# A hybrid decoder layer: ranking the mixer's hops and the evictions, and moving four ties and loads

## The chip, the cores and the metric

The kernel is one program on one core of a Trainium2 chip. Time is the device time of one execution in microseconds, the median of repeated runs. The core has five engines with queues of their own: TensorE (PE, matmuls into PSUM; its weight loads are shown as PEld), VectorE (DVE), ScalarE (ACT), GpSimd (POOL) and SyncE (SP), which here issues nearly every DMA. Instructions of one engine run in the order in which they stand in its queue. Semaphores order the engines among each other.

## What is computed

One decoder layer on 2048 tokens of width 1024, in float32:

```python
mod = jax.nn.silu(c) @ w_ada + b_ada
shift1, scale1, gate1, shift2, scale2, gate2 = jnp.split(mod, 6, axis=-1)
h = modulate(rmsnorm(x, norm1_w), shift1, scale1)
q, k, v, z, xbc, dt = split(h @ w_in)
attn = sliding_window_attention(rope(q), rope(k), v, sinks)      # 8 heads, window 128
xbc = silu(causal_depthwise_conv(xbc, conv_w, conv_b))           # 4 taps
y = ssd_chunked_scan(xs, softplus(dt + dt_bias), A, B, C, d_skip) # 16 chunks of 128, a state carried
y = grouped_rmsnorm(y * silu(z)) * ssm_norm_w
x = x + gate1 * (concat(attn, y) @ w_out)
h = modulate(rmsnorm(x, norm2_w), shift2, scale2)
x = x + gate2 * ((silu(h @ w_gate) * (h @ w_up)) @ w_down)
return rmsnorm(x, final_norm_w)
```

## The kernel before

**Numbers.** Each float32 factor of a projection is split into a high half, rounded to fp32r (ACT, a copy), and a low half (DVE, the difference). A product is then three matmuls, hi x hi, hi x lo and lo x hi (`mm3`, L281 to L284). Weights are loaded to `raw`, split into `w` (six buffers), and for later blocks the split form is kept in DRAM.

**Blocks and projections.** The tokens are worked in four blocks of 512, b = 0 to 3. For each block the stage before the feed-forward part runs, one after another on PE: `queries`, `keys_values`, `convolved` (8 columns of 128 channels) and `gated`. Each computes into a PSUM bank `d` (four of them, from `dense()`), and evicts: `query` and `key_value` apply the rotary angles (`rope`, DVE and POOL) and store to DRAM; `gate` applies silu and stores; `convolved` evicts a column by a copy of the bank with its three halo columns (L510), two scaled copies on ACT (L513, L514), two multiply-adds on DVE (L515, which reads the bank, and L516) and a sum on POOL (L517). The tail of a column, `end` (L491 to L494: a Tanh, a multiply-add and the store of the column), is traced half a column later.

**The mixer beside them.** `attentions(b)` and `ssds(b)` are generators. One step of them, between two yields, is a hop: a few small matmuls or transposes on PE in banks am, at, sm and st, and the vector work that answers them. `tick` (L1473) advances such a side generator by a given ratio between the steps of the main one. Their results go to DRAM (`spill`). In `attentions` a hop is, in turn: transposes of k and q (L611, L616), scores and their maxima (L651, L660), the softmax (L669 to L679), its transposes (L685, L687) and the product with v (L694, L696). In `ssds` it is: transposes of x (L752), the product of B and C (L759), decays (L723 to L728), the state's output (L785), the new state (L794), the output (L806 to L809), a root mean square whose inverse square root takes some fifteen tiny instructions on DVE and POOL (L815, `rsqrt` at L246), and, hops later, the scaling on ACT (L734), the transposes (L739) and the store (L742, L743). They load q, k, v, z and x of the next 128 tokens on SP one tile ahead (L599, L600, L702, L703).

**Other work in the same queues.** `norm1` of the next block loads x twice (L363, and L345 in `load_x`), squares it on ACT (L364), and makes the operands `hl` (L337, L339, L340). `ada_later` computes the rest of `mod` by reductions on DVE (L204). `mixed(b)` loads the mixer's result from `spill` (L831) and splits it into halves (L837 on ACT, L839 on DVE). `out_proj(b)` multiplies it by w_out, adds x (L858), stores (`mid`, L859) and sums squares. It loads x of column c + 1 in the middle of column c.

**The feed-forward part.** Gate and up projection are done by a Strassen-like scheme: `quads(s)` for token blocks 2s and 2s + 1, 22 quads of seven products each (L1034 to L1036), with operands made by `operands_first`, `operands_between`, `sums_ahead`, `operands_kept` and `operands_last`. The down projection follows the same scheme (`steps_of`, L1166; its token operands `a` at L1147 and L1148, its weights at L1161 and L1162). During the first quads the hops of blocks 2 and 3 run as sides; then `first_output` and `second_output` project blocks 2 and 3, and `first_operands` and `last_operands` run as sides too.

**Order.** A scheduler at build time goes through the traced instructions with a model of the machine. On each engine it takes, of those that are ready in the model, the one of the lowest rank. The rank is the place in the trace. On PE the order is the traced one from the opening through the last projection of block 3; from the first quad on PE is ranked as well. Inside `tc.manual_schedule` other engines named there keep the traced order too. `tc.issue_after(i)` ties what is traced in it behind instruction i in the queue of i's engine, without a wait for its end; `behind(engine)` (L189) ties to the last instruction traced on that engine. In the kernel before, `mixed` ties both halves of its split in this way.

Of the kernel before, what the change touches and what calls it, by code (L numbers as in the profile page):

```python
# [18 lines left out]
P = 128  # L19
# [12 lines left out]
RAW, SPLIT = 5, 6  # L32
TMP, M1, M2, M4 = 8, 3, 8, 4
MIX, MIX2, MIX1, RATIO_UP = 0.78, 1.1, 1.25, 0.75
HALF = 32
ROPE_THETA = 10000.0
TWO_PI_1 = 6.25
# [7 lines left out]
def hymba_layer(ctx, tc, xT, xtok, pos, wada, wadk, vecs, rows, wq, wkv, wz, wx, wo, wgu, wd, outT):  # L45
# [139 lines left out]
        nc.vector.scalar_tensor_tensor(scl1[:, d:d + 2], mod[:, 8 + d:10 + d], 1.0, n1w[:, d:d + 2], ALU.add, ALU.mult)  # L185

    held_back = set()

    def behind(engine):  # L189
        traced = nc.cur_bb.bb.instructions  # L190
# [236 lines left out]
    def two_parts(b, h, name, src, done):  # L427

        store, banks = b == (0 if name == "z" else 1), [None, None]
        for kh in range(2):  # L430
            for part in range(2):
                if kh == 0:
                    banks[part] = [dense(), dense()]
                outs = [banks[part][t // 2][:, t % 2 * 256:t % 2 * 256 + 256] for t in range(NT)]
                for kp in (2 * kh, 2 * kh + 1):
                    whi, wlo = weight(src[part][kp], 512, (f"{name}{part}", kp), store)
                    for e in range(2):
                        k, cs = 2 * kp + e, slice(e * 256, (e + 1) * 256)
                        for t, out in enumerate(outs):
                            ts = slice(t * P, (t + 1) * P)  # L440
                            mm3(out, h[k][0][:, ts], h[k][1][:, ts], whi[:, cs], wlo[:, cs],
                                k == 0 and t % 2 == 0, k == KT - 1 and t % 2 == 1)
                    if kp % 2 == 0:
                        yield
                if kh:
                    for t, out in enumerate(outs):
                        done(part, t, out)
                yield

    def first_columns(h):  # L450
# [29 lines left out]
    def keys_values(b, h, halves=(0, 1), bank_of=lambda i: dense()):  # L480
        if b and 0 in halves:
            dt_of[b] = small([P, NT, 8], "dt", 3)
        for half in halves:
            for t, ps in (yield from tokens(b, h, "kv", wkv, 264, (2 * half, 2 * half + 1), bank_of)):
                key_value(b, t, ps)
            yield

    def convolved(b, h):
        ending = []

        def end(c, cv, th, o):  # L491
            nc.scalar.activation(th, cv, AF.Tanh)
            nc.vector.scalar_tensor_tensor(o, th, 1.0, cv, ALU.add, ALU.mult)
            nc.sync.dma_start(xs_d[b][c], o)  # L494

        for c in range(8):
            ps = dense()
            for half in range(2):
                if half:
                    if ending:  # L500
                        end(*ending.pop())
                    yield
                whi, wlo = weight(wx[c, half], T, ("x", c, half), b == 1)
                for i in range(4):
                    k = 4 * half + i
                    ws = slice(i * P, (i + 1) * P)
                    mm3(ps, whi[:, ws], wlo[:, ws], h[k][0], h[k][1], k == 0, k == KT - 1)
            cin = small([P, T + 3], "cin", 2, pool=ip)
            nc.gpsimd.tensor_copy(cin[:, 0:3], halo[:, c, :])
            nc.scalar.copy(cin[:, 3:T + 3], ps)  # L510
            nc.gpsimd.tensor_copy(halo[:, c, :], cin[:, T:T + 3])
            cv, th, o = big("s", 3, pool=fw), big("s", 3, pool=fw), big("sx", 2, pool=ip)
            nc.scalar.activation(cv, cin[:, 0:T], AF.Identity, scale=conv_w[:, c, 0:1], bias=conv_b[:, c:c + 1])  # L513
            nc.scalar.activation(th, cin[:, 1:1 + T], AF.Copy, scale=conv_w[:, c, 1:2])  # L514
            nc.vector.scalar_tensor_tensor(cv, ps, conv_w[:, c, 3:4], cv, ALU.mult, ALU.add)  # L515
            nc.vector.scalar_tensor_tensor(th, cin[:, 2:2 + T], conv_w[:, c, 2:3], th, ALU.mult, ALU.add)  # L516
            nc.gpsimd.tensor_tensor(cv, cv, th, ALU.add)  # L517
            ending.append((c, cv, th, o))
            if c == 7:
                end(*ending.pop())  # L520
            yield
# [305 lines left out]
    def mixed(b, mix, cs, into):  # L827
# [5 lines left out]

        def split():
            for n, (hi, lo) in enumerate(got):
                with behind(mybir.EngineType.Activation):
                    nc.scalar.activation(hi, lo.bitcast(F32), AF.Copy)  # L837
                with behind(mybir.EngineType.DVE):
                    nc.vector.tensor_tensor(lo, lo.bitcast(F32), hi.bitcast(F32), ALU.subtract)  # L839
                mix.append((hi, lo))  # L840
                if n % 2:
                    yield
        return split()

    def out_proj(b, y_of, mix, bank_of, acc, norm=None, each=lambda c: None):
        nxt = load_x(b, 0)
        for c in range(KT):
            ps, x = bank_of(c), nxt
            for half in range(2):
                if half:  # L850
                    nxt = load_x(b, c + 1) if c < KT - 1 else None
                    yield
                whi, wlo = weight(wo[c, half], T, ("o", c, half), b == 0, b > 1)
                for i in range(4):
# [618 lines left out]
    def tick(ratio):  # L1473
# [7 lines left out]
        due[0] += ratio  # L1481
        while due[0] >= 1.0:
            due[0] -= 1.0
            while sides and next(sides[0], sides) is sides:
                sides.pop(0)

    def beside(main, ratio):
        for i, _ in enumerate(main):
# [309 lines left out]
```

## Time and profile before

| what | us |
|---|---|
| median of three runs | 2225.2 (2223.36 to 2226.75) |
| the profiled execution | 2224.71 |
| its span, first to last instruction | 2223.0 |
| mean granted PE clock | 0.987 |
| POOL busy | 549.9 |
| opening, to the first projection on PE | about 36 |
| projections and mixer, blocks 0 to 3, up to the first quad | about 36 to 711 |
| first quads; the hops of blocks 2 and 3 beside them up to 1211 | about 711 to 1272 |
| output projections of blocks 2 and 3 | about 1218 to 1337 |
| first part of the down projection | about 1338 to 1434 |
| second quads | about 1435 to 1865 |
| the rest of the down projection and the final norm | about 1857 to 2223 |

A row of the stretches names an interval, its length, then busy time and number of instructions of each engine, then the granted clock of PE (1.00 is full), the DMA share and its rate. In a row of a timeline stand the start, the duration, the engine, the line, the operation, what it writes and reads, the shape, and in brackets how long the engine had been idle and what ended that. "SPq" is the issuing of DMAs in SP's queue. "w L882 <- PE d L1036: 226.7, 124, 4.8" would read: ACT waited for PE 226.7 us in total, 124 times, at most 4.8 us.

### The profile page before, as it was taken

The page shows a single profiled execution, that of the slowest core. Times are in us where ns is not written, and L with a number is a line of the kernel's source. Part 1 is how long each engine was busy: PE and PEld are TensorE (multiplying, and loading weights), DVE is VectorE, ACT ScalarE, POOL GpSimd, SP SyncE. Part 2 cuts the span into 40 slices and gives each one's busy share as a digit, 9 for nine tenths or more (in the row PEclk, how much of TensorE's full clock was granted, in tenths as well). Part 3 has the DMA queues.
Part 4 walks back from the last instruction along what each step waited for, and adds up shares of the span by engine and source line. Part 5 has one row for each costly group of instructions (what it writes and reads, how often), then busy time and mean ns, then how long its engine had stood idle before and what let it go on. Part 6 is the DMA issues. An engine that isn't in the chain of part 4 may idle for free.

```text
span 2223.0 us, 33256 instructions
## 1 busy us (share of the span) xinstructions
PE 2154.6 (97%) x10984; PEld 1775.6 (80%) x10984; DVE 1660.7 (75%) x3195; ACT 1017.4 (46%) x2135; POOL 549.9 (25%) x658
## 2 busy tenths in 40 slices
PE   8989999999899999999998999999999999999998
PEld 6879897778678677788887888788888888788887
DVE  6977856876568777688886878878878775786575
ACT  3664734743445555433343545533333333554451
POOL 0213443322102211144342221233232231110011
PEclk9989999999999999999999999999999999999999
DMA  7788988796899432333333587835555535778653
GB/s 271 248 306 279 353 263 282 255 320 198 305 339 357 150 106 86 104 119 105 125 122 119 199 296 252 279 125 166 189 162 187 168 118 202 257 261 271 180 170 102
DMA packets 287708, 466.76 MB, mean 210 GB/s; under 512 B 27440, under 2 KB 97072, under 8 KB 287536
## 3 DMA queue, kind: packets, MB, share of 16 engines
q1 hardware_dynamic: 286960, 464.13, 62.6%
q8 instruction: 86, 1.41, 0.3%
q14 instruction: 86, 0.70, 0.1%
q10 hardware_dynamic: 576, 0.52, 0.1%
HBM read 329.73 MB, written 134.81 MB: 209 GB/s over the span
## 4 chain that ended last, share of the span: by engine, by line
PE 88%; DVE 4%; DMA 4%; ACT 2%; issue 1%; POOL 0%; SPq 0%; DVEq 0%; ACTq 0%; POOLq 0%
PE d L1166 15%; PE d L1034 10%; PE d L1036 10%; PE d L1035 10%; PE d L282 7%; PE d L283 7%; PE d L284 7%; PE d L1307 1%; PE am L1036 1%; PE am L1034 1%; PE am L1035 1%; PE am L694 1%; PE sm L806 1%; DMA a<-act_t 1%; PE sm L1036 1%
## 5 line engine op out<-in xcount | busy, mean ns | idle before, releaser
L1166 PE MATMUL d<-a,w 128*128 128x512 f32 x1716 | 403.4, 396 | 3.8 <-DVE w L1162 2.0
L1166 PEld LDWEIGHTS d<-a,w 128*128 128x128 f32 x1716 | 321.7, 188 | 82.6 <-DVE w L1162 2.9
L1034 PE MATMUL d<-b,w 128*128 128x512 f32 x924 | 365.6, 400 | 4.4 <-ACT b L916 2.1
L1035 PE MATMUL d<-b,w 128*128 128x512 f32 x924 | 367.3, 397 | 0.3 <-DVE b L917 0.2
L1036 PE MATMUL d<-b,w 128*128 128x512 f32 x924 | 367.3, 398 | 0.0
L1034 PEld LDWEIGHTS d<-b,w 128*128 128x128 f32 x924 | 174.5, 189 | 44.3 <-ACT b L916 2.6
L1035 PEld LDWEIGHTS d<-b,w 128*128 128x128 f32 x924 | 174.8, 189 | 41.0 <-DVE b L917 1.1
L1036 PEld LDWEIGHTS d<-b,w 128*128 128x128 f32 x924 | 174.0, 188 | 40.3 <-issue 0.4
L882 ACT ACTIVATE w<-s 128x512 fp32r<-128x512 f32 x176 | 110.8, 631 | 204.4 <-PE d L1036 160.1
L282 PE MATMUL d<-w,hl 128*128 128x256 f32 (+1 forms) x592 | 174.6, 295 | 7.6 <-DVE s L515 6.7
L283 PE MATMUL d<-w,hl 128*128 128x256 f32 (+1 forms) x592 | 169.2, 286 | 0.0
L284 PE MATMUL d<-w,hl 128*128 128x256 f32 (+1 forms) x592 | 169.1, 286 | 0.0
L883 DVE TENSOR_TENSOR w<-s,w 128x512 fp32r<-128x512 f32 x176 | 159.5, 908 | 7.6 <-ACT w L882 6.8
L1148 DVE TENSOR_TENSOR a<-a 128x512 fp32r<-128x512 f32 x154 | 109.7, 725 | 52.2 <-ACT a L1147 52.1
L882 ACT ACTIVATE w<-raw 128x512 fp32r<-128x512 f32 x132 | 83.4, 632 | 137.8 <-PE d L1036 66.6
L1162 DVE TENSOR_TENSOR w<-raw,w 128x512 fp32r<-128x512 f32 x156 | 112.4, 729 | 41.7 <-ACT w L1161 41.5
L1147 ACT ACTIVATE a<-a 128x512 fp32r<-128x512 f32 x154 | 96.0, 628 | 94.9 <-DMA a<-act_t 57.0
L282 PE MATMUL d<-hl,w 128*128 128x512 f32 x320 | 133.4, 417 | 2.6 <-ACT hl L837 2.6
L292 POOL TENSOR_TENSOR acc<-acc,t 128x512 f32<-128x512 f32 x35 | 54.4, 1554 | 322.3 <-ACT t L291 311.4
L1161 ACT ACTIVATE w<-raw 128x512 fp32r<-128x512 f32 x156 | 90.9, 588 | 87.6 <-PE d L1166 56.1
L283 PE MATMUL d<-hl,w 128*128 128x512 f32 x320 | 127.1, 397 | 1.0 <-DVE hl L839 1.0
L284 PE MATMUL d<-hl,w 128*128 128x512 f32 x320 | 127.3, 398 | 0.0
(421 smaller groups left out, 4787.4 us busy)
## 6 DMA issues: line engine op xcount, KB each, us to landing
raw<-in_wgu_dram SPq DMA_DIRECT2D x176, 256.0 KB, 2.9
act_t<-t SPq DMA_DIRECT2D x88, 256.0 KB, 3.3
a<-act_t SPq DMA_DIRECT2D x88, 256.0 KB, 4.3
act_b<-t SPq DMA_DIRECT2D x66, 256.0 KB, 2.1
a<-act_b SPq DMA_DIRECT2D x66, 256.0 KB, 4.2
aw<-in_wada_dram SPq DMA_DIRECT2D x64, 256.0 KB, 4.7
w<-w_x SPq DMA_DIRECT2D x32, 512.0 KB, 5.8
raw<-wd_s SPq DMA_DIRECT2D x64, 256.0 KB, 3.1
```

The costliest lines, as they stand in the source:

```text
L282: nc.tensor.matmul(out, ahi, bhi, start=first, stop=False)
L283: nc.tensor.matmul(out, ahi, blo, start=False, stop=False)
L284: mm3.last = nc.tensor.matmul(out, alo, bhi, start=False, stop=last)
L882: nc.scalar.activation(hi, x, AF.Copy)
L883: eng.tensor_tensor(lo, x, hi.bitcast(F32), ALU.subtract)
L1034: nc.tensor.matmul(out, ahi, bhi, start=first and k == 0, stop=False, skip_group_check=True)
L1035: nc.tensor.matmul(out, ahi, blo, start=False, stop=False, skip_group_check=True)
L1036: mm3.last = nc.tensor.matmul(out, alo, bhi, start=False, stop=k == 3, skip_group_check=True)
L1147: nc.scalar.activation(hi, raw, AF.Copy)
L1148: nc.vector.tensor_tensor(lo, raw, hi.bitcast(F32), ALU.subtract)
L1162: nc.vector.tensor_tensor(w[1], raw, w[0].bitcast(F32), ALU.subtract)
L1166: mm3.last = nc.tensor.matmul(ps, w[x][:, ws], act[k][y], start=new and k == 0 and x + y == 0, stop=k == KP - 1 and x == 1, skip_group_che ...
```

## The change

`urgent()` opens `tc.high_priority(1000)`: what is traced in it gets a rank lower by 1000, so it stands in the ranking where an instruction traced 1000 instructions earlier stands. It holds every step of a side generator in `tick`, the evictions of queries and gates in `two_parts`, `key_value` in `keys_values`, and the evictions of `convolved`, which move to a function of their own, with L515's operation traced before L514's. Work called from `pending`, from `finish`, or by plain iteration is not in it.

In `convolved` the tail's Tanh and multiply-add are now tied behind the last instruction traced on ACT and on DVE; its store is not. In `mixed` the two halves of the split lose their ties. In `out_proj` blocks 2 and 3 load x in the middle of the column that uses it; blocks 0 and 1 keep the load a half column before the column begins.

```diff
+URGENT = 1000
...
+    def urgent():
+        return tc.high_priority(URGENT)
...
                 if kh:
-                    for t, out in enumerate(outs):
-                        done(part, t, out)
+                    with urgent():
+                        for t, out in enumerate(outs):
+                            done(part, t, out)
...
-                key_value(b, t, ps)
+                with urgent():
+                    key_value(b, t, ps)
...
         def end(c, cv, th, o):
-            nc.scalar.activation(th, cv, AF.Tanh)
-            nc.vector.scalar_tensor_tensor(o, th, 1.0, cv, ALU.add, ALU.mult)
+            with behind(mybir.EngineType.Activation):
+                nc.scalar.activation(th, cv, AF.Tanh)
+            with behind(mybir.EngineType.DVE):
+                nc.vector.scalar_tensor_tensor(o, th, 1.0, cv, ALU.add, ALU.mult)
             nc.sync.dma_start(xs_d[b][c], o)
+
+        def evicted(c, ps):
+            cin = small([P, T + 3], "cin", 2, pool=ip)
+            nc.gpsimd.tensor_copy(cin[:, 0:3], halo[:, c, :])
+            nc.scalar.copy(cin[:, 3:T + 3], ps)
+            nc.gpsimd.tensor_copy(halo[:, c, :], cin[:, T:T + 3])
+            cv, th, o = big("s", 3, pool=fw), big("s", 3, pool=fw), big("sx", 2, pool=ip)
+            nc.scalar.activation(cv, cin[:, 0:T], AF.Identity, scale=conv_w[:, c, 0:1], bias=conv_b[:, c:c + 1])
+            nc.vector.scalar_tensor_tensor(cv, ps, conv_w[:, c, 3:4], cv, ALU.mult, ALU.add)
+            nc.scalar.activation(th, cin[:, 1:1 + T], AF.Copy, scale=conv_w[:, c, 1:2])
+            nc.vector.scalar_tensor_tensor(th, cin[:, 2:2 + T], conv_w[:, c, 2:3], th, ALU.mult, ALU.add)
+            nc.gpsimd.tensor_tensor(cv, cv, th, ALU.add)
+            return c, cv, th, o
...
-            ending.append((c, cv, th, o))
+            with urgent():
+                ending.append(evicted(c, ps))
...
             for n, (hi, lo) in enumerate(got):
-                with behind(mybir.EngineType.Activation):
-                    nc.scalar.activation(hi, lo.bitcast(F32), AF.Copy)
-                with behind(mybir.EngineType.DVE):
-                    nc.vector.tensor_tensor(lo, lo.bitcast(F32), hi.bitcast(F32), ALU.subtract)
+                nc.scalar.activation(hi, lo.bitcast(F32), AF.Copy)
+                nc.vector.tensor_tensor(lo, lo.bitcast(F32), hi.bitcast(F32), ALU.subtract)
...
     def out_proj(b, y_of, mix, bank_of, acc, norm=None, each=lambda c: None):
-        nxt = load_x(b, 0)
+        nxt = load_x(b, 0) if b < 2 else None
...
                 if half:
-                    nxt = load_x(b, c + 1) if c < KT - 1 else None
+                    if b > 1:
+                        x = load_x(b, c)
+                    else:
+                        nxt = load_x(b, c + 1) if c < KT - 1 else None
...
         while due[0] >= 1.0:
             due[0] -= 1.0
-            while sides and next(sides[0], sides) is sides:
-                sides.pop(0)
+            with urgent():
+                while sides and next(sides[0], sides) is sides:
+                    sides.pop(0)
```

More of the change, by code (lines that the diff above doesn't have):

```diff
@@ L507, in convolved @@
                     mm3(ps, whi[:, ws], wlo[:, ws], h[k][0], h[k][1], k == 0, k == KT - 1)
[L508 to L517, printed above, removed]
-            ending.append((c, cv, th, o))
+            with urgent():
+                ending.append(evicted(c, ps))
             if c == 7:
```

## The prediction

> **What bounds the kernel now.** I read the page first, then the table of 50-us stretches, then the waits of PE alone, then short timelines around the longest of them. The page:
>
> ```profile
> span 2223.0 us, 33256 instructions
> PE 2154.6 (97%) x10984; PEld 1775.6 (80%) x10984; DVE 1660.7 (75%) x3195; ACT 1017.4 (46%) x2135; POOL 549.9 (25%) x658
> ```
>
> TensorE is the bound: idle for 2223.0 - 2154.6 = 68.4 us only. The edit adds and removes no matmul, so it can win at most what PE loses by waiting. The stretches (columns: length; busy us and count of PE, PEld, DVE, ACT, POOL; granted clock; DMA share; GB/s) say where that is:
>
> ```profile
> 100.00:150.00 50.00, 39.75 (x248) 35.13 (x246) 42.57 (x104) 36.67 (x84) 14.36 (x18) 0.93 0.88 306
> 350.00:400.00 50.00, 45.31 (x224) 36.27 (x223) 35.52 (x81) 23.13 (x50) 16.24 (x21) 0.93 0.73 243
> 400.00:450.00 50.00, 44.35 (x317) 39.37 (x315) 40.14 (x95) 35.48 (x95) 16.63 (x24) 0.97 0.84 275
> 500.00:550.00 50.00, 45.11 (x335) 40.67 (x334) 30.18 (x100) 20.91 (x59) 10.58 (x27) 0.97 0.60 192
> 550.00:600.00 50.00, 41.76 (x249) 34.23 (x250) 34.33 (x123) 23.85 (x59) 11.26 (x25) 0.93 0.91 331
> 1500.00:1550.00 50.00, 50.00 (x217) 40.59 (x216) 39.88 (x56) 16.55 (x28) 15.07 (x10) 1.00 0.52 165
> 750.00:1210.00 460.00, 460.00 (x2224) 372.16 (x2222) 360.24 (x626) 198.77 (x450) 136.97 (x158) 1.00 0.33 107
> ```
>
> The undisturbed row gives the price of one 128x512 matmul: 50 us / 217 = 0.230 us. Five stretches of the projections with the mixer beside them lose 10.25 + 4.69 + 5.65 + 4.89 + 8.24 = 33.7 us of PE, the 460 us of quads nothing at all. Where PE idles, the clock column falls below 1.00 too. PE's own waits (us in total, times, longest), longest first:
>
> ```profile
> PE st L739 <- ACT m L734: 10.7, 3, 4.6
> PE d L282 <- DVE s L515: 6.7, 1, 6.7
> PE d L282 <- ACT b L837: 6.5, 1, 6.5
> PE am L282 <- ACT mo L1645: 5.8, 1, 5.8
> PE at L616 <- DMA m<-q: 3.3, 1, 3.3
> PE d L282 <- ACT hl L837: 2.6, 1, 2.6
> ```
>
> These six are 35.6 us, and the edit touches the releaser of five of them directly. What the clock costs behind a wait:
>
> ```profile
> 366.60:371.40 4.80, 4.80 (x14) 3.82 (x15) 0.00 (x0) 1.47 (x5) 0.00 (x0) 0.50 0.67 218
> 426.00:434.00 8.00, 5.98 (x51) 5.07 (x50) 7.21 (x20) 5.48 (x13) 4.78 (x12) 1.00 0.86 289
> 446.00:450.00 4.00, 4.00 (x11) 3.06 (x11) 3.46 (x8) 0.22 (x1) 0.00 (x0) 0.57 1.01 367
> 597.60:603.50 5.90, 5.90 (x13) 4.40 (x14) 1.69 (x5) 3.72 (x12) 0.00 (x0) 0.50 0.00 0
> ```
>
> After the 6.5 us wait the 13 matmuls of 597.6 to 603.5 take 5.9 us instead of 13 x 0.230 = 3.0: 2.9 us more, at half clock. After 4.6 us it is 4.8 / 2 = 2.4 us, after the 2.6 us wait and its 1.0 us successor 4.0 - 11 x 0.230 = 1.5 us; the 2.0 us wait inside 426 to 434 left the clock at 1.00.
>
> The Trainium skill, TensorE: Matmul & The Clock Gate, section Why this matters for your kernels, says to allow no PE gap over about 3 us between bursts. By it a wait that shrinks under that length gives its clock term back in full; the 446 us row, where gaps of 2.6 and 1.0 us halved the clock, says that this is not sure. The sum below would be 3 us better by the rule.
>
> **The change, part by part.** Durations are of the profiled execution, which took 2224.71 us: 1.7 us around the span, and 0.5 us below the median of 2225.2.
>
> *Convolution evictions ranked forward.* ACT, DVE and PE around 130 us:
>
> ```profile
> 122.50 0.57 ACT L510 COPY cin<-d 128x512 f32<-128x512 f32 x1
> 125.15 0.63 ACT L364 ACTIVATE t<-t 128x512 f32<-128x512 f32 x1 [1.25 <-DMA t<-in_xtok_dram]
> 129.37 0.80 ACT L513 ACTIVATE s<-cin,vec 128x512 f32<-128x512 f32 x1
> 130.20 0.75 DVE L515 SCALAR_TENSOR_TENSOR s<-d,vec,s 128x512 f32<-128x512 f32 x1
> 131.00 0.58 PE L282 MATMUL d<-w,hl 128*128 128x256 f32 x1 [6.65 <-DVE s L515]
> ```
>
> The bank's copy L510 is done at 123.1, but its partner L513 runs at 129.37, behind squares (L364) of the next block's norm which wait for their transfers. With the eviction ranked first, L513 (0.80) and L515 (0.75) end near 124.7, or 125.3 behind one ACT instruction of 0.63; PE came at 131.0 - 6.65 = 124.35. So 5.7 to 6.3 us of the 6.65 go, plus about 2 us of half clock. I take -7; ends 0 (something else arrives late) and -9. The norm work that is overtaken has its cover: the whole gate projection, 192 matmuls, lies between it and the projection that reads it. Without the cover it would be late by what passes it, some 2 us a column.
>
> *The mixer's hops ranked forward: loads.* Two rows of SP, and one of the table of transfers (KB, us to landing):
>
> ```profile
> 143.57 1.32 SPq L345 DMA_DIRECT2D t<-in_xT_dram  x2
> 144.94 0.43 SPq L600 DMA_DIRECT2D m<-q  x1
> t<-in_xT_dram SPq DMA_DIRECT2D x56, 256.0 KB, 5.2
> ```
>
> PE's 3.3 us for q end on a load that SP issued behind two loads of x which are only prefetch. Ranked first it goes at least 1.4 us sooner, but PE itself will now come 7 us sooner. I take -3; ends 0 and -6 (3.3 and a clock term). Every load and store of a hop now passes the weights' loads in SP's queue, 0.4 us of issue each; six split weights of 12 matmuls, 16.6 us, lie ready to hide it, and without them each would cost PE its 0.4.
>
> *The mixer's hops: the chain to L739.* Before the third of these waits:
>
> ```profile
> 504.91 0.40 ACT L813 ACTIVATE m<-m 128x256 f32<-128x256 f32 x1
> 507.44 1.23 DVE L340 SCALAR_TENSOR_TENSOR hl<-t,mod,hl 128x512 fp32r<-128x512 f32 x1
> 508.93 0.15 DVE L815 TENSOR_SCALAR ss<-ss 128x2 f32<-128x2 f32 x1
> 517.64 1.04 PE L739 MATMUL st<-ident,m 128*128 128x128 f32 x4 [4.14 <-ACT m L734]
> 362.97 0.74 DVE L204 CUSTOM_DVE_ANT_0 aw<-aw,csil,vec 128x512 f32<-128x512 f32 x1
> ```
>
> The sum is ready at 505.4 and its tiny L815 runs at 508.9 behind norm operands (L340) that nobody needs yet: 3.5 us. At 363 two ada reductions (L204) of 0.74 sit in the chain of the first: 1.5 us. For the one of 2.0 us I take 1. All these are ranked behind now. 3.5 + 1.5 + 1 = 6 of 10.7, and with them the clock terms of the 4.1 and 4.6 us waits, 2 and 2.4: I take -10; ends 0 and -15. What is late next is the rsqrt's own chain of some 15 tiny instructions, which no ranking shortens.
>
> *Halves of the projection's operand untied (L837, L839).*
>
> ```profile
> 442.14 1.74 ACT L679 ACTIVATE m<-m,ast 128x256 f32<-128x256 f32 x4
> 443.74 1.18 ACT L837 ACTIVATE hl<-hl 128x512 fp32r<-128x512 f32 x2
> 590.68 1.14 ACT L837 ACTIVATE b<-b 128x512 fp32r<-128x512 f32 x2
> 595.32 1.69 ACT L679 ACTIVATE m<-m,ast 128x256 f32<-128x256 f32 x4
> 596.91 1.13 ACT L837 ACTIVATE b<-b 128x512 fp32r<-128x512 f32 x2
> 597.58 0.80 PE L282 MATMUL d<-b,w 128*128 128x512 f32 x1 [6.51 <-ACT b L837]
> ```
>
> In both places PE waits for a pair that stands directly behind the softmax scaling L679, the last ACT instruction traced before it: the tie made the wait. Free, the pair at 596.91 can follow the one at 590.68; given as long again for its DVE half it is ready near 593, so 4.5 of 6.5 us go and 2.9 of clock with them. The pair at 443.74 stands behind the same instruction: 2.6 + 1.0 + 1.5 go. I take -12; ends +4 (rival C) and -14.
>
> *Quads and output stage.* PE's order is held by hand only up to the first quad. After it PE is ranked too. The 5.8 us at 1211 are such a place: PE stands at the first matmul of block 2's output projection, whose tile has still to be stored, loaded and split, with quads left to run. Hops moved forward end the scan sooner and can hide that behind quads: with a clock term of 2 behind it, up to -8. The price is that PE meets every hop as soon as the planner thinks it ready, not later. I take -6 for the first and +6 for the second (rival B bounds it), net 0.
>
> *Conv tails tied, L515 traced before L514.* L492 (0.63), L493 (0.73) and the store run later. No instruction of PE waits for them before the scan reads the block; nothing is queued behind the tied Tanh but work ranked lower or already issued. 0 with that cover; without it the scan's load, at 5.2 us like x's, once in each of four blocks, +21 at most. *x loaded later for blocks 2 and 3*: the load is issued 12 matmuls or 2.8 us before its use and a load of x takes 5.2 us, so the eviction comes 2.4 us late: 16 x 2.4 = 39 us if nothing hid it, but the other bank takes the next column of 24 x 0.230 = 5.5 us. 0. *Query, key and gate evictions forward*: none of PE's long waits ends on them, POOL, which has their sums, is at 25%. 0, ends +2 and -2. *Operands of the second quads forward*: they take DVE from the down projection's splits, where DVE was busy 65.65 of 80 us:
>
> ```profile
> 1330.00:1410.00 80.00, 78.57 (x339) 62.55 (x338) 65.65 (x110) 41.81 (x76) 14.74 (x10) 1.00 0.82 274
> ```
>
> PE loses 1.4 us there now; I take +3, ends 0 and +10.
>
> Sum: -7 - 3 - 10 - 12 + 0 + 3 = -29. I give a quarter back, since PE arriving some 30 us sooner meets loads that did not move: of the 35.6 us, 3.3 + 5.8 = 9.1 end on a transfer already, a quarter. 2224.7 - 29 + 7.3 = 2203.0: **2203 us**, -1.0%.
>
> **The rivals.**
> A, *waits replaced*: each hop shortened lets PE run into the next thing, as into q's load behind L515; the tie's 12 us and half of the other 20 stay away, against the far end of the operands: 2224.7 - 12 - 10 + 10 + 7.3 = 2220. For it: DMA share 0.88 and 0.91 in the two worst stretches. Against: ACT is busy 46%.
> B, *slower*: in the quads PE's order now follows the ranking, with no slack between a hop's vector work and its next matmuls. By the code there are some 104 such phases in 750 to 1210: 8 token tiles x 9 of the scan, 4 x 8 of the attention. They decide from (29 - 7.3 + 6) / 104 = 0.27 us each; at 0.4, in place of the 6 in the sum, 2224.7 - 29 + 7.3 - 6 + 42 = 2239, at 0.5 2249. For it: PE has no wait at all there now, so anything is a loss. Against: already now PE meets hops whose chain is longer than their spacing, and waits 0.0 us.
> C, *free halves block ACT*: they may be put ahead of evictions before their loads have landed:
>
> ```profile
> DMA to landing us min/median/max: 3.5/5.6/7.9
> ```
>
> A block of up to 7.9 us in each of two places, less the 12 no longer won: 2203 + 12 + 2 to 8 = 2217 to 2223. It would take back what the tie's end gives and little more. By the Trainium skill, PSUM — Partial Sum Buffer, section Engine vs sequencer instructions, the ScalarE and VectorE queues are strict FIFO; the 1.25 us that ACT stood at L364 with evictions behind it agrees.
> D, *the ranking changes almost nothing*, because what is ready first still goes first: only half of the tie's 12 us: about 2219.
>
> **How the numbers follow.** Forecast 0.64 (its own range 2189 to 2217), A 0.10, B 0.16, C 0.06, D 0.04. About 0.2%, 4.5 us, is what a measurement of this kernel can tell. Within it of 2225.2 (2220.7 to 2229.7) lie most of A, half of C, some of D and the near end of B, 0.16; slower is the rest of B, 0.13; faster 0.71. All good ends together, -9 - 6 - 15 - 14 - 8 = -52, would be 2173; a twentieth lies below 2184. The range leaves that out and B beyond some 0.3 us: 2184 to 2230.
>
> **What would show it.** Right: the L515 wait near 124 under 1 us; no pair L837 directly behind L679 and PE's waits for L837 under 3 us together; L815 within 1 us of its sum; the 100 to 600 us rows with 20 us more PE; the clock at 1.00 in most of them. Wrong: PE idle inside the 460 us of quads (B); ACT standing at L837 for a transfer (C); new waits of PE on transfers in the projections (A); the same six waits (D).

## The result and the profile after

The changed kernel takes 2202.7 us (median of 4 runs, 2201.4 to 2204.9) against 2224.3 us of the kernel before (4 runs, 2220.5 to 2226.8): a ratio of 0.9905, 95% interval 0.9888 to 0.9923. The forecast of 2203 us holds. Two of its larger terms did not come, though, and others made up for them, in part by luck.

Most lines moved: before's L204 is now L208, L282 to L284 are L286 to L288, L600 is L612, L345 is L349, L510, L513, L514, L515 are L507, L510, L512, L511, the tail L492, L493 is L499, L501, L734 and L739 are L746 and L751, L806 is L818, L815 is L827, the halves L837 and L839 are L848 and L849. The head of the page after:

```profile
span 2203.2 us, 33249 instructions
...
PE 2149.3 (98%) x10984; PEld 1771.8 (80%) x10984; DVE 1661.3 (75%) x3195; ACT 1014.0 (46%) x2135; POOL 550.6 (25%) x658
```

The span is 19.8 us shorter: 5.3 us less of busy PE (the same 10984 matmuls, less of them at half clock) and 14.5 us less of idle PE (53.9, was 68.4). The waits of PE after (us in total, times, longest):

```profile
PE st L751 <- ACT m L746: 11.8, 2, 7.5
PE d L286 <- DVE s L511: 6.5, 1, 6.5
...
PE d L287 <- DVE b L849: 1.6, 2, 1.3
PE am L286 <- DVE t L871: 1.5, 1, 1.5
...
PE at L628 <- DMA m<-q: 0.9, 1, 0.9
```

The two waits the ranking was to remove stand at the head of the list, as long as before (10.7 and 6.7). Gone are the waits for the tied halves (10.5 in all, now 1.6), the one at 1211 (5.8), and most of that for q (3.3). The stretches after (columns as before):

```profile
100.00:200.00 100.00, 91.93 (x666) 84.77 (x665) 76.86 (x220) 60.81 (x152) 27.36 (x45) 0.97 0.86 301
350.00:400.00 50.00, 42.48 (x203) 33.90 (x203) 35.12 (x80) 24.77 (x59) 16.05 (x20) 0.90 0.67 222
400.00:450.00 50.00, 48.17 (x349) 42.82 (x348) 40.74 (x99) 35.01 (x91) 16.12 (x25) 1.00 0.84 274
550.00:600.00 50.00, 47.50 (x255) 37.50 (x254) 34.70 (x104) 25.68 (x62) 9.32 (x14) 1.00 0.98 349
600.00:750.00 150.00, 144.36 (x794) 115.73 (x793) 111.65 (x247) 84.37 (x201) 28.79 (x28) 0.95 0.85 295
750.00:1210.00 460.00, 459.80 (x2212) 371.76 (x2212) 366.22 (x626) 203.71 (x458) 131.87 (x158) 1.00 0.35 114
1210.00:1300.00 90.00, 88.52 (x385) 71.29 (x384) 57.62 (x96) 39.15 (x67) 19.32 (x13) 1.00 0.66 220
```

and those of before that the prediction does not show:

```profile
600.00:750.00 150.00, 144.00 (x803) 115.35 (x803) 105.41 (x241) 82.13 (x192) 24.31 (x27) 0.97 0.88 304
...
1210.00:1300.00 90.00, 84.20 (x360) 67.37 (x359) 63.89 (x90) 43.61 (x77) 18.75 (x12) 0.96 0.70 235
```

Read PE's busy column and the clock together. At 400 to 450 and 550 to 600, where the halves had been late, the clock is back at 1.00 and PE gains 3.8 and 5.7 us. At 350 to 400 it loses 2.8 us more than before and the clock falls to 0.90. The quads of 750 to 1210 lose 0.2 us. At 600 to 750 the clock fell from 0.97 to 0.95.

Such rows compare different work, since the changed kernel is further on. Up to the first quad PE takes the same matmuls in the same order in both kernels, so the start of one and the same matmul says how far ahead the changed kernel is (matmuls of L282 to L284; in the last row but one the first of the quads, in the last the end of the span):

| before, us | what lies just ahead of it | changed kernel ahead, us |
|---|---|---|
| 36.2 | the opening | 1.8 |
| 143.1 | the wait for L515 | 1.1 |
| 157.8 | the wait for q | 7.1 |
| 358.2 | | 6.0 |
| 380.7 | the first wait on L739 | 2.6 |
| 434.8 | the second wait on L739 | 3.1 |
| 472.0 | the halves near 442 | 8.6 |
| 568.3 | the third wait on L739 | 9.6 |
| 605.1 | the halves near 591 | 17.5 |
| 710.7 | | 17.5 |
| 2223.0 | the end | 19.8 |

The first 1.8 us are not the change's: the opening is the same in both, and in the fourteen profiled executions of this document the first projection starts anywhere from 34.1 to 36.5 us.

### The profile page after: what moved, and what is told of

The parts are those of the page before. It is cut to its first block, busy times and chain, and to the rows that moved or that the text cites. A ratio compares the mean times of both kernels' runs of the same rounds, so it can differ in the third digit from the quotient of the medians.

```text
span 2203.2 us, 33249 instructions
## 1 busy us (share of the span) xinstructions
PE 2149.3 (98%) x10984; PEld 1771.8 (80%) x10984; DVE 1661.3 (75%) x3195; ACT 1014.0 (46%) x2135; POOL 550.6 (25%) x658
## 4 chain that ended last, share of the span: by engine, by line
PE 84%; DVE 7%; DMA 5%; issue 2%; ACT 2%; POOL 1%; SPq 0%; DVEq 0%; ACTq 0%; POOLq 0%
PE d L1179 18%; PE d L1049 9%; PE d L1048 9%; PE d L1047 9%; PE d L286 6%; PE d L288 6%; PE d L287 6%; PE d L1320 1%; PE am L1049 1%; PE am L1047 1%; PE am L1048 1%; PE am L706 1%; PE sm L1049 1%; PE sm L1047 1%; PE sm L1048 1%
## 5 line engine op out<-in xcount | busy, mean ns | idle before, releaser
L286 PE MATMUL d<-w,hl 128*128 128x256 f32 (+1 forms) x592 | 173.7, 293 | 6.9 <-DVE s L511 6.5
L288 PE MATMUL d<-w,hl 128*128 128x256 f32 (+1 forms) x592 | 168.2, 284 | 0.0
L896 DVE TENSOR_TENSOR w<-s,w 128x512 fp32r<-128x512 f32 x176 | 156.7, 891 | 10.1 <-ACT w L895 9.4
L286 PE MATMUL d<-hl,w 128*128 128x512 f32 x320 | 133.2, 416 | 0.0
L288 PE MATMUL d<-hl,w 128*128 128x512 f32 x320 | 127.0, 397 | 0.3 <-DVE w L279 0.3
```

The source lines that it names most:

```text
L286: nc.tensor.matmul(out, ahi, bhi, start=first, stop=False)
L288: mm3.last = nc.tensor.matmul(out, alo, bhi, start=False, stop=last)
L896: eng.tensor_tensor(lo, x, hi.bitcast(F32), ALU.subtract)
```

## The experiments

Twelve kernels, each timed beside the kernel before. Four began as that kernel with one part of the change, three as the changed kernel with one part undone, five add something to test a cause. T is the theory of an expectation and R its rival.

**One part alone.** The halves without the tie:

```diff
-                with behind(mybir.EngineType.Activation):
-                    nc.scalar.activation(hi, lo.bitcast(F32), AF.Copy)
-                with behind(mybir.EngineType.DVE):
-                    nc.vector.tensor_tensor(lo, lo.bitcast(F32), hi.bitcast(F32), ALU.subtract)
+                nc.scalar.activation(hi, lo.bitcast(F32), AF.Copy)
+                nc.vector.tensor_tensor(lo, lo.bitcast(F32), hi.bitcast(F32), ALU.subtract)
```

> The kernel before with one edit: the halves of the output projection's operand (L837, L839) no longer tied. Theory T, each part of the change keeps its own gain: the waits of 6.5, 2.6, 1.0 and 0.4 us on those lines fall to about 1.5 and their half-clock stretches go with them: -12 us, so about 2212; the waits on L734 (10.7), L515 (6.7) and L1645 (5.8) stay within 1 us. Rival R, the halves are early only because the evictions and hops they would block are ranked ahead of them: alone they put ACT behind a transfer and the time moves by less than 4 us.

Measured: 2216.5 us, ratio 0.9975 (0.9966 to 0.9984), -5.5 us at the 2223 of before by the ratio and -6.9 by the medians. Its waits (the halves are L836 on ACT and L837 on DVE here):

```profile
PE st L739 <- ACT m L734: 10.0, 2, 6.0
...
PE am L282 <- ACT mo L1643: 6.0, 1, 6.0
...
PE at L616 <- DMA m<-q: 4.1, 1, 4.1
PE sm L759 <- DVE m L808: 3.9, 1, 3.9
...
PE d L283 <- DVE b L837: 3.0, 3, 1.9
```

The halves' own waits fell as expected, 10.5 to 3.0 us; 4.7 us of that came back, as a new wait of 3.9 us for L808 near 419 and 0.8 us more for q. The wait on L734 near 362 grew from 4.55 to 6.0. The time lies between T and R, nearer to R. The hops ranked alone (the `with urgent()` in tick and nothing else):

> The kernel before with one edit: the hops issued by tick ranked 1000 forward. Theory T: the wait of 5.8 us at 1211 goes with its half clock (-8) and the wait for q falls from 3.3 to about 1 (-2); the waits on L734 stay near 10 us and those on the tied halves (10 us) stay: about 2214. Rival R1, the wait at 1211 went through x being loaded later, not through the ranking: then it stays and the time is about 2222. Rival R2, hops ranked alone push the tied halves later still: over 2225.

Measured: 2221.4 us, 0.9991 (0.9982 to 1.0000): R1's time, but not its reason, and between T and R2. The wait for mo has left the list, as T said; the one for q has not, and the tied halves got later, as R2 said:

```profile
PE d L286 <- ACT b L841: 8.0, 1, 8.0
PE d L286 <- ACT hl L841: 7.3, 1, 7.3
...
PE at L620 <- DMA m<-q: 4.0, 2, 3.8
```

The 7.3 us in a timeline (ACT and DVE of this kernel; L732 here is before's L728, L683 and L680 are L679 and L676):

```profile
443.69 1.75 DVE L732 TENSOR_TENSOR m<-m,m 128x512 f32<-128x512 f32 x1
445.36 0.17 DVE L680 RECIPROCAL ast<-ast 128x4 f32<-128x4 f32 x1
...
445.62 1.70 ACT L683 ACTIVATE m<-m,ast 128x256 f32<-128x256 f32 x4 [2.69 <-DVE ast L680]
447.23 1.13 ACT L841 ACTIVATE hl<-hl 128x512 fp32r<-128x512 f32 x2
```

ACT stands 2.69 us at the softmax scaling for a tiny reciprocal that sits behind L732 on DVE, and the tied pair is next behind it. A tie makes a late hop's lateness PE's. The evictions ranked alone (with L515's operation traced before L514's, as in the change):

```diff
+                    with urgent():
+                        for t, out in enumerate(outs):
+                            done(part, t, out)
...
+                with urgent():
+                    key_value(b, t, ps)
...
+            with urgent():
+                ending.append(evicted(c, ps))
```

> The kernel before with the evictions of query, gate, key and convolution ranked 1000 forward and L515 traced before L514; nothing else. Theory T: the wait of 6.7 us at 124 to 131 stays, since the order of ACT there did not change in the changed kernel either; no other long wait of PE ends on an eviction: within 4 us of the kernel before. Rival R, the ranking of the evictions is what kept them ahead of the untied halves and of the norm, and alone it already gives 5 us or more.

Measured: 2220.0 us, 0.9983 (0.9975 to 0.9992), inside T. The wait at 124 to 131 is 7.5 us, not shorter, but the one for q has gone from the list: it was these evictions, not the hops, that ended it (which of them was not tried). The later loads of x alone:

```diff
-        nxt = load_x(b, 0)
+        nxt = load_x(b, 0) if b < 2 else None
...
-                    nxt = load_x(b, c + 1) if c < KT - 1 else None
+                    if b > 1:
+                        x = load_x(b, c)
+                    else:
+                        nxt = load_x(b, c + 1) if c < KT - 1 else None
```

> The kernel before with one edit: for blocks 2 and 3 the output projection loads x after the first half of its column instead of a column ahead. Theory T, the wait of 5.8 us at 1211 was that of a PE order in which the first matmuls of block 2's output projection stand too early, and any edit that lets the planner put more of the quads ahead of them removes it, this one too: the wait goes with its half clock, -8 us, 2215 to 2216. Rival R, in the changed kernel without ranked hops it went by the free halves or the evictions: then it stays here and the time is within 3 us of the kernel before.

Measured: 2219.0 us, 0.9975 (0.9965 to 0.9986), T's wait but 4.8 us instead of its 8. PE in the kernel before, then here:

```profile
1217.63 0.79 PE L282 MATMUL am<-mo,w 128*128 128x512 f32 x1 [5.80 <-ACT mo L1645]
```

```profile
1221.14 0.50 PE L282 MATMUL am<-mo,w 128*128 128x512 f32 x1 [0.81 <-ACT mo L1648]
```

The wait for mo fell from 5.8 to 0.8 us, by an edit that touches neither that tile nor its loads. Those did not come sooner: SP issues the first at 1216.9, in the kernel before at 1214.0. But between the last transposes of the scan (L739, which start at 1213.5 here and at 1210.5 before) and these matmuls PE now works through 6.3 us of quads instead of 0.7. So two parts of the change remove the wait, each alone, and two leave it (6.0 us with the halves free, 5.8 with the evictions ranked). Here it went by where the planner put those matmuls among the quads; with the hops ranked the scan itself ends sooner (its last transposes start at 1192.5 in that kernel).

**One part undone.** The changed kernel with the halves tied as before:

> The changed kernel with one edit undone: the halves tied again. Theory T: the time goes back by the 12 us of the ties, about 2214 to 2215, with waits of PE on the two lines of the halves of some 8 to 10 us. Rival R, hops ranked forward leave ACT free earlier so the tie costs less than it did: under 5 us, about 2206.

Measured: 2217.5 us, 0.9978 (0.9969 to 0.9987), 14.8 us above the changed kernel. The same edit that is worth 5.5 to 6.9 us alone is worth two to three times that in company:

```profile
PE d L286 <- ACT hl L849: 7.3, 1, 7.3
...
PE d L286 <- ACT b L849: 5.3, 1, 5.3
```

The hops left unranked (tick as before):

> The changed kernel without the ranking of the hops issued by tick; all other edits stay. Theory T, the hops' ranking is worth the wait of 5.8 us at 1211 with its clock (8 us together) and nothing in the projections, where the q wait fell by the evictions' ranking and the long waits by the free halves: about 2211. Rival R1, the free halves only pay with the hops ranked (free alone gave 5.5 us where undoing them costs 14.8): 2216 or more, with waits of PE for halves or for the hops they pass. Rival R2, later loads of x removed the wait at 1211: under 2206.

Measured: 2198.4 us, 0.9891 (0.9876 to 0.9905), against 0.9905 (0.9888 to 0.9923) with the ranking: no worse, perhaps 3 to 4 us better, though the intervals overlap. R2 comes nearest. Where that may lie, by windows, first of the changed kernel, then of this one:

```profile
700.40:710.60 10.20, 9.82 (x29) 7.79 (x28) 8.99 (x22) 4.64 (x14) 1.04 (x1) 0.50 0.75 273
```

```profile
700.20:703.60 3.40, 2.82 (x7) 2.24 (x8) 3.40 (x12) 1.05 (x3) 0.00 (x0) 0.50 1.03 367
```

In the first quads the changed kernel runs at half clock for 10.2 us, this one for 3.4: (10.2 - 3.4) / 2 = 3.4 us. Another 3.4 us at half clock (from 727.7) and the wait of 1.5 us at 1260 are gone too, 1.7 and 1.5 us: together about the 6.5 us by which the two profiled spans differ. The waits at 356, 504 and 122 are the same in both (7.6, 4.2, 6.7 here), and the 1211 wait stays away by the later x. The tails untied:

> The changed kernel with one edit undone: the convolution's tail (L499, L501) no longer tied. Theory T, the tie costs and gives nothing, as the prediction put it: within 2.5 us of the changed kernel (2200 to 2205), the waits at 122, 356 and 504 as they were. Rival R, the tie holds the tail and with it the buffer of L512 and the vector queue ahead of L820: without it the wait at 122 falls by 2 us or more and the time below 2200.

Measured: 2205.6 us, 0.9915 (0.9901 to 0.9928): T, within the noise; the wait at 124 is no shorter (7.7 us). Smaller waits are new, though: 5.8 us on L697 (its L699 in the changed kernel has 3.1) and 2.8 us on L818.

**Causes of the two waits that stayed.** At 122 to 129 the changed kernel's ACT shows the tail of the column before, then the two ACT parts of the eviction; L512 needs a buffer which that tail's DVE part L501 frees:

```profile
124.89 0.62 ACT L499 ACTIVATE s<-s 128x512 f32<-128x512 f32 x1
...
126.86 0.70 ACT L512 ACTIVATE s<-cin,vec 128x512 f32<-128x512 f32 x1
127.47 0.80 ACT L510 ACTIVATE s<-cin,vec 128x512 f32<-128x512 f32 x1
```

```diff
-            cv, th, o = big("s", 3, pool=fw), big("s", 3, pool=fw), big("sx", 2, pool=ip)
+            cv, o = big("s", 3, pool=fw), big("sx", 2, pool=ip)
+            th = big("s4", 1, pool=ip) if c % 2 else big("s", 3, pool=fw)
...
-        return small([P, 256], "so", 6, pool=ip)
+        return small([P, 256], "so", 5, pool=ip)
```

> The changed kernel with one edit: the odd columns of the convolution take th from a buffer of their own (the staging tiles so go from 6 to 5 to make room), so that two columns can be in flight. Theory T, the wait of 6.5 us at 122 to 129 is not one of rank but of a buffer: L512 of a column needs the buffer that the tail L499, L501 of the column before frees, and the tail stands behind squares waiting for transfers: with a buffer more the wait falls under 1.5 us and its half clock goes: -6 to -8 us against the changed kernel's 2203, so 2195 to 2197. Rival R, the eviction's ACT part stands behind the squares in any case: the wait stays over 5 us and the time within 2 us of 2203.

Measured: 2198.2 us, 0.9885 (0.9871 to 0.9900), an interval that still touches the changed kernel's. The wait fell to 4.0 us, half of what T said. ACT's part now ends before PE needs it, but L512 (before's L515) stands in DVE's queue instead:

```profile
119.89 0.80 ACT L511 ACTIVATE s<-cin,vec 128x512 f32<-128x512 f32 x1
```

```profile
122.15 2.41 DVE L344 SCALAR_TENSOR_TENSOR hl<-t,mod,hl 128x512 fp32r<-128x512 f32 x2
124.48 1.28 DVE L279 TENSOR_TENSOR w<-raw,w 128x512 fp32r<-128x512 f32 x2
125.69 0.73 DVE L512 SCALAR_TENSOR_TENSOR s<-d,vec,s 128x512 f32<-128x512 f32 x1
```

So the buffer was one holder and DVE's order the next. Its windows:

```profile
100.00:200.00 100.00, 95.09 (x671) 87.64 (x670) 82.68 (x229) 61.61 (x153) 38.30 (x44) 0.95 0.89 308
600.00:750.00 150.00, 145.39 (x826) 116.67 (x824) 116.57 (x260) 87.17 (x205) 29.12 (x29) 0.99 0.85 294
```

At 100 to 200 PE is busy 3.2 us more than in the changed kernel, but at clock 0.95 for 0.97: less 0.02 x 100, 1.2 us won. Most of the 4.5 us is at 600 to 750 again, clock 0.99 for 0.95: near 700 it has 3.4 us at half clock where the changed kernel has 13.7.

The wait near 356. In the changed kernel ACT stood at a free half for its load, rival C's mechanism:

```profile
348.12 0.63 ACT L848 ACTIVATE hl<-hl 128x512 fp32r<-128x512 f32 x1 [5.57 <-DMA hl<-mix]
```

```diff
+        anchor = next(i for i in reversed(nc.cur_bb.bb.instructions)
+                      if i.engine == mybir.EngineType.Activation and i.name not in held_back)
...
+                with tc.issue_after(anchor) if b == 0 and n < 4 else nullcontext():
                     nc.scalar.activation(hi, lo.bitcast(F32), AF.Copy)
```

> The changed kernel with one edit: the first four of the eight ACT halves of block 0's operand may not be issued before the last ACT instruction traced when the operand is set up, some 65 us later; the others stay free. Theory T, the free halves made ACT stand 5.57 us at 342 to 348 for a transfer and held the hop's chain back by 3 us: PE's wait on L746 near 356 falls from 7.5 to about 4.5 us and its half-clock stretch from 10.24 to 6.83: -4 to -5 us, 2198 to 2199. Rival R, the wait at 356 is the chain of the rsqrt with lower-ranked work in its gaps, whatever ACT does at 342: it stays over 6.5 us and the time within 2 us of 2203.

Measured: 2202.7 us, 0.9909 (0.9894 to 0.9924). T's wait, R's time. PE in the changed kernel, then here; L818 is the product that starts the chain, L751 the transposes that read its end:

```profile
348.52 1.89 PE L818 MATMUL sm<-m,m 128*128 128x64 f32 x16
...
363.52 1.11 PE L751 MATMUL st<-ident,m 128*128 128x128 f32 x4 [7.53 <-ACT m L746]
```

```profile
351.58 1.89 PE L818 MATMUL sm<-m,m 128*128 128x64 f32 x16
...
363.61 1.09 PE L751 MATMUL st<-ident,m 128*128 128x128 f32 x4 [4.55 <-ACT m L746]
```

Both waits end at the same time, but PE came here 3 us later, to L818 already. What counts is the time from L818 to L751, since PE starts the chain itself: 15.0 us in the changed kernel, 12.0 here, with the same 7.5 us of other matmuls between the two. So ACT's stand, and the halves that run on ACT and DVE right behind it, held the chain up by 3.0 us, as T said, and the half clock behind the wait fell from 10.2 to 3.4 us. That the time stayed is another matter. Of the 3 us 1.5 were lost in the opening, which this edit does not touch, and 0.9 at the wait near 124 (7.3 us for 6.5); and behind the chain a new wait of 2.25 us on L746 at 429.5, with half clock after it, took some 3.4 us back. Whether those follow from the edit is open. One tick more ahead of it:

```diff
             out = (y, o, ts, rs)
             yield
         yield
+        yield
         normed(out[0], out[3])
```

> The changed kernel with one edit: at the end of each block of the scan one tick more between the root mean square and the transposes L751 that need it. Theory T, what PE waits for there is a chain of fixed length that rank can't shorten, so only distance helps: the 7.5 us near 356 falls to about 4.7 and the 4.3 us near 504 (a token tile inside its block, which this edit doesn't touch) stays: -3 to -6 us with the clock, 2197 to 2200. Rival R, the tick is eaten because the chain's vector work is issued later with it: the wait stays over 6 us, time within 2 us of 2203.

Measured: 2196.8 us, 0.9877 (0.9860 to 0.9893), an interval that still touches the changed kernel's. T in its time and for 356 (3.4 us left: 10.2 us of matmuls between L818 and L751 for 7.5, and a chain of 13.6 us, as ACT stood 4.16), but the wait at 504 went as well, which neither theory had:

```profile
350.00:400.00 50.00, 46.64 (x234) 37.76 (x233) 39.10 (x88) 26.25 (x57) 17.55 (x23) 0.93 0.77 256
500.00:550.00 50.00, 49.38 (x402) 45.76 (x402) 29.12 (x132) 19.85 (x62) 12.10 (x29) 1.00 0.75 254
```

The tick moves every later hop by one against the projections; that this is what freed 504 was not tried by itself.

**Together.** Unranked hops, the tick and the buffer:

> The changed kernel with three edits together: the hops not ranked, one tick more at the end of each block of the scan, a buffer of its own for th of the odd columns. Theory T, the three gains lie in different places except near 700 (-4.3 with 5.5 of it near 700, -5.9 with 4 near 700, -4.5 with 5 near 700): 2.5 from 122, 4.6 from 356, 5.4 from 504 and 5 from 700, about 2186. Rival R, the waits at the first quads come and go with every shift of the order and the token tiles' chains fall elsewhere on PE's order: 2193 or more, with new waits on L746 or in the quads.

Measured: 2194.6 us, 0.9868 (0.9854 to 0.9881), an interval wholly below the changed kernel's: faster than both kernels. But the three gains of 4.3, 5.9 and 4.5 us do not add; they gave 8.2. Unranked hops and the buffer had each brought the half clock near 700 from 13.7 to 3.4 us, worth some 5, which can be won once; the rest is within the noise of the three. R is the nearer. In this kernel's chain L266, 0.16 us elsewhere, is long once, as in the kernels above (DVE, then POOL):

```profile
360.30 1.21 DVE L266 SCALAR_TENSOR_TENSOR rs<-rss,rs 128x2 f32<-128x2 f32 x1
```

```profile
359.80 1.70 POOL L515 TENSOR_TENSOR s<-s 128x512 f32<-128x512 f32 x1 [2.19 <-DVE s L514]
```

L266 ends when POOL's sum does (361.5). With that sum on DVE:

```diff
-            nc.gpsimd.tensor_tensor(cv, cv, th, ALU.add)
+            nc.vector.tensor_tensor(cv, cv, th, ALU.add)
```

> The kernel of the run before (no ranked hops, one tick more, buffer for th) with one edit: the sum of cv and th that ends a convolution column runs on DVE (32 more instructions of 0.68 us there) instead of POOL (1.3 to 1.7 us each). Theory T, a DVE instruction with both operands in SBUF stands still while such a POOL sum runs: L266, tiny at 0.16 us, took 1.21 us at 360.30 and ended with POOL's sum at 361.50; without the sum the chain to L747 is 1.05 us shorter, PE's wait near 358 falls from 4.8 to 3.8 us or less, and DVE's busy time rises by less than 32 x 0.68 = 22 us: 2190 to 2194 against 2194.6. Rival R, DVE is the next bound in the projections (48.06 of 50 us at 100 to 150): the sums come between splits that PE needs, new waits on the splits of weights, 2198 or more.

Measured: 2191.8 us, 0.9866 (0.9850 to 0.9883): not to be told from the run before, and just as surely faster than both kernels. The wait on L747 fell from 4.8 to 3.8 us as T said, L266 takes 0.15 us, and the wait at 124 is back at 5.8, behind squares on ACT. By the pages DVE was busy 1670.3 us in the run before and is busy 1665.9 here: it has 32 instructions of 0.68 us more and is busy 4.4 us less. By this difference some 26 us of its busy time had been standing still beside POOL.

## Why the prediction held, and where its steps did not

- **Halves untied, -12: right**, in place and size, where they were late. Their waits fell by 8.9 us, and the lead of the changed kernel grows by 5.5 us near 442 and by 7.9 near 591: 13.4 in all. That the edit needs the rest of the change to pay in full (5.5 to 6.9 alone) the prediction did not see, nor what it costs near 356 (below).
- **Evictions of the convolution, -7: wrong.** The wait is 6.5 us, and 0.7 us of the lead go. The step that failed is "With the eviction ranked first, L513 (0.80) and L515 (0.75) end near 124.7": it took the squares alone for the holder. The eviction's partner had to have a buffer, and behind that a place on DVE; rank gives neither. That is half of the wait at most: with the sum on DVE the ACT parts came behind squares again, buffer or not, and what makes the planner choose so stays open.
- **q's load, -3: right about the holder, too low, and wrong about what would lift it.** The wait went from 3.3 to 0.9, with the half clock of 149.5 to 156.3 behind it: 6.0 us. The two loads of x (L349) no longer stand ahead of q's on SP:

```profile
140.76 0.48 SPq L612 DMA_DIRECT2D m<-q  x1
...
150.29 1.71 SPq L349 DMA_DIRECT2D t<-in_xT_dram  x2
```

  But that came with the ranked evictions, which had been given nothing for it; the ranked hops alone left q's load at 144.99, behind two loads of x, and the wait at 4.0.
- **The chain to L739, -10: wrong.** The waits are 11.8 us, and near 356 the change costs 3.4 us. The step that failed is "All these are ranked behind now". Ranking the hops did nothing for the chain of the first wait. In the kernel before it starts at

```profile
354.55 1.89 PE L806 MATMUL sm<-m,m 128*128 128x64 f32 x16
...
366.58 1.12 PE L739 MATMUL st<-ident,m 128*128 128x128 f32 x4 [4.55 <-ACT m L734]
```

  and takes 12.0 us from L806 to L739. It takes 12.0 with the hops ranked alone, too, and 12.0 in the changed kernel with the halves tied, each time with a wait of 4.55 us. Other work still runs inside it, on DVE of the changed kernel:

```profile
358.51 0.75 DVE L511 SCALAR_TENSOR_TENSOR s<-d,vec,s 128x512 f32<-128x512 f32 x1
...
359.91 0.74 DVE L208 CUSTOM_DVE_ANT_0 aw<-aw,csil,vec 128x512 f32<-128x512 f32 x1
...
360.58 1.21 DVE L266 SCALAR_TENSOR_TENSOR rs<-rss,rs 128x2 f32<-128x2 f32 x1
```

  With L513 at 359.25 and another L208 at 361.72, each 0.74, these stand between links of the chain (the first link at 357.20, the last ends at 362.92), in the order that the kernel before has too; and L266, a link, stands still beside the sum of that eviction on POOL. L511 and L513 belong to an eviction, which the change ranks forward just as far as the hop, so the ranking does not move the hop past them. L208 is not ranked and still came in between. That the planner took the next link for not yet ready there is likely, but not shown: with nothing between them the links follow one another in 0.2 us. What made the chain longer than before, 15.0 us, are the free halves. Near 504 the wait stayed (4.26 us for 4.14): the sum is ready at 496.0, and its L827 runs at 498.8, behind norm operands as before. Only the 2.0 us wait went.
- **Quads, net 0: the wait at 1211 went, as forecast, and most of it was lost elsewhere.** That wait and the half clock behind it cost 5.8 + 1.9 = 7.7 us (PE worked through 3.7 us of that half clock). But from the first quad to the end the lead grows by 2.3 us only, 17.5 to 19.8: half clock near 700 to 731 is 13.7 us, where it was 6.8 near 740 (some 3.5 us), and a wait of 1.5 is new at 1260. The +6 of rival B did not come: PE is busy 459.80 of 460 us. And the cause was not the ranking alone, since x alone does it.
- **Operands of the second quads, +3: too high.** With everything 20 us earlier the stretch of 1310 to 1390 has PE busy 79.32 of 80 us: 0.7 us lost, where it was 1.4.
- **A quarter given back, +7: right in sign and near in size, not in reason.** It was taken for PE meeting unmoved loads. What came back was 3.4 us at 356, 3.5 near 700, 1.5 at 1260 and 0.7 near 124. Of these only the first has to do with a load, and there it was ACT that met it.
- **Rivals.** C came true in one place: ACT stood 5.57 us for a load, and with the halves behind it that made the chain to L751 3.0 us longer. A came true in the experiments, where each cure met the next holder; at 356 PE's earlier coming was not the cause, since PE itself starts the chain. B did not come. D's reason, that what is ready first still goes first, fits what became of the terms of -7 and -10. The sum held by luck as much as by reason: -13.4, -6.0 and -7.7 (for -12, -3 and 0) stood in for the -7 and -10 that did not come, and 9.1 came back where +7 and +3 had been allowed. That is -18.0, and the opening's 1.8 make it the 19.8 of the two profiled spans.
- **The signs named for it.** Two came: no half stands directly behind the softmax scaling, and PE's waits for the halves are under 3 us together (1.6). The others failed: the wait near 124 is 6.5 us and not under 1, L827 runs 2.8 us after its sum near 504 and not within 1, the rows of 100 to 600 have 9.6 us more PE (475.28 for 465.68) and not 20, and of the five stretches of the projections that the prediction lists, those of 400 to 450 and 550 to 600 alone have the clock at 1.00. Of the signs against it C's was there, ACT standing at a half for a transfer.

## What to carry to other kernels

A rank did nothing here for an instruction that waited for something else: before giving it credit, look for what the late one waits for (a buffer, a queue, the link before it), and whether what stands ahead of it is ranked just as far. Expect a chain of tiny instructions to be filled with other work; more distance between the chain and its reader helped where rank did not. Measure such a chain from the matmul of PE that starts it to the one that reads its end, and not by the time at which the wait ends. A tie to "the last instruction traced" puts its work behind any wait that this instruction has, so work with a reader near by is better left free; but free work can put its own wait, here for a load, ahead of others in the queue. And when one part of a change is timed alone or undone alone, the two answers can differ by a factor of two to three; give both.

## What the hardware showed that was not expected

DVE stands still beside POOL. Of the 308 splits L896 of the changed kernel (0.68 us each, both operands in SBUF), the 218 that no POOL instruction overlaps all take 0.70 us or less; of the 90 that one overlaps, 59 take over 0.89 us, up to 1.79. The products L402 and L403, which read PSUM, are not slowed: in 128 overlaps the longest takes 0.41 us, without one 0.43. The Trainium skill, SBUF — State Buffer, section Who interferes with whom, says so: a DVE instruction with two SBUF inputs contends with a GpSimd instruction that reads SBUF, and the second blocks. The 1.21 us of L266 agrees: POOL's sum began first, and L266 ended with it.

The clock halves without a long wait. In the changed kernel's first quads it was 0.50 from 700.4 to 710.6 us though PE waited at most 0.92 us at a time just before; in the kernel with unranked hops, with one wait of 1.34 us there, it lasted 3.4 us. These stretches, worth 1.7 us for each 3.4, moved with nearly every edit, which is one reason why small gains near 700 neither add up nor can be planned from a profile.
